# A mixture of 16,384 one-neuron experts on one core: one gather of 8 KB rows per choice, one-hots weighted on VectorE

## The chip, the cores and the metric

The kernel runs on one core of a Trainium2 chip. The core has a matrix engine (TensorE: PE, and PEld for its weight loads), a vector engine (VectorE, DVE), an activation engine (ScalarE, ACT), GpSimd (POOL), and SyncE (SP), which issues most transfers. Each engine works through its own list of instructions in order, and the lists meet only at semaphores. The metric is the time of one execution on the device, in microseconds (us); lower is better.

## The reference

The program is a network of three blocks in float32 over 512 tokens of 1024 features. The change touches only the experts that close the first block. Each of 8 heads picks the best 16 of 128 x 128 experts for a token, so each token has 128 experts; an expert is one row u and one row v of 1024 numbers:

```python
def peer_ffn(a, w_q, sub_keys, u_tab, v_tab):
    qry = (af @ w_q).reshape(n, PEER_HEADS, 2, PEER_KEY_DIM)
    s = jnp.einsum('nhpd,hpkd->nhpk', qry, sub_keys).astype(jnp.float32)
    s_top, i_top = lax.top_k(s, PEER_TOPK)
    cand = (s_top[:, :, 0, :, None] + s_top[:, :, 1, None, :]).reshape(n, PEER_HEADS, PEER_TOPK * PEER_TOPK)
    sc, ci = lax.top_k(cand, PEER_TOPK)
    e_a = jnp.take_along_axis(i_top[:, :, 0], ci // PEER_TOPK, axis=-1)
    e_b = jnp.take_along_axis(i_top[:, :, 1], ci % PEER_TOPK, axis=-1)
    experts = e_a * PEER_N_KEYS + e_b
    gw = jax.nn.softmax(sc, axis=-1)
    ...
        u = u_tab[eb]
        act = jax.nn.gelu(jnp.einsum('td,tkd->tk', xb, u).astype(jnp.float32), approximate=False)
        wts = (gb * act).astype(v_tab.dtype)
        return jnp.einsum('tk,tkd->td', wts, v_tab[eb])
```

## The kernel before

**Two ways to the same sum.** The first 128 tokens (tile 0) are done sparsely: for each of a token's 128 choices the row u is gathered and multiplied with the token (a *dot*, L1508, on DVE), and later the row v is gathered and added with its weight (an *add*, L1513, on DVE). One gather (L1495, issued by POOL) fetches 128 rows, one per token. The other 384 tokens (tiles 1 to 3) are done densely: all 16,384 experts are computed for all of them, 128 experts at a step. A *u-step* computes gelu(u x) (24 matmuls of 384 columns), a *v-step* adds v times the weighted result into six accumulators (18 matmuls of 512). Between the two, the result `at` is multiplied by `gt`, which holds for each expert and token the weight, or zero for an expert that was not chosen.

**How G, the table of weights, is made.** For four tokens at a time DVE writes a one-hot `oa` of each choice's upper index and a one-hot `ob` of the lower (L1609), POOL multiplies `ob` by the weights (L1611), and PE forms four 128 x 128 products in `pa` (L247), which ACT copies to `gs`; 16 tokens of it go to memory `gd` at once. 384 tokens make 96 such groups of four.

**Products.** Each float32 product is three passes over a high and a low part. The weight (512 KB a step) arrives as `wr`, ACT writes its high part `wh` (L227), DVE subtracts to get `wl` (L228); one such subtract a u-step and one a v-step, so 256 in all here. The weighted result is split in the same way, `pwh` on ACT and `pwl` on DVE.

**Two stages.** In the first, 64 of the 128 u-steps run (results to memory) while `peer_select` makes the choices and G: for each head and tile `cand` (L1556) and its 16 largest by two rounds of MAX8, FIND_INDEX8 and MATCH_REPLACE8, then for each half of a choice a decode (L1583 to L1589). In the second, 128 v-steps run with the other 64 u-steps and the gathers: first 64 turns of u and v together (a *pair*), then 64 of v alone. In what follows a *unit* is one u-step or one v-step. At the end `entry` adds the accumulators to x, normalises each tile, transposes it, and begins the next block.

**Who sets the order.** Program order is only a proposal: the scheduler of the block writes out each engine's list by a model of its own, so steps of `peer_gathered`, `peer_select` and the u-steps can be moved past each other within the limits of the pools (`oh`, `pg`, `gr`, `vw` and so on give the number of buffers).

Of the kernel before, what the change touches and what calls it, by code (L numbers as in the profile page):

```python
# [9 lines left out]
F32 = mybir.dt.float32  # L10
F32R = mybir.dt.float32r
BF16 = mybir.dt.bfloat16
# [9 lines left out]
T = 512  # L22
NT = 4
# [64 lines left out]
def pack(I):  # L88
# [35 lines left out]
    g["peer_ur"] = a["peer_u"][0]  # L124
# [49 lines left out]
class Build:  # L174
# [1224 lines left out]
    def peer(self, x, xa, xr, dst):  # L1399
# [13 lines left out]
        with self.pools(pr=1, gr=3) as (pr, gr):  # L1413
            sel = {k: pr.tile([128, 128], d, name=f"sel_{k}") for k, d in (("g", F32), ("e", I32), ("w", F32))}
            with self.pools(pk=1) as pk:
# [8 lines left out]
                with self.pools(uo=3) as uo:  # L1424
                    fill = self.peer_select(vals, idx, iob, gd, sel)
                    for e in range(split):
# [7 lines left out]
            sparse = self.peer_gathered(x, xr, sel, gr)  # L1434
            self.banks(pl=2, pa=0, po=0, pt=0, pv=6)
            acc = [self.psum("pv") for _ in range(6)]
            with self.pools(vg=2, va=2, vw=5) as (vg, va, vw):
                gts, ats, ws = {}, {}, {}

                def first(e):  # L1440

                    if e % 8 == 0:
                        gts[0] = vg.tile([128, n // 16, 8, 16], F32, name="gt")
                        nc.sync.dma_start(gts[0], gd[:, :, e:e + 8].rearrange("c b a t -> b c a t"))
# [8 lines left out]
                    nc.gpsimd.tensor_mul(av, av, gts[0][:, :, e % 8])  # L1453
# [26 lines left out]
            if dst is not None:  # L1480
                self.entry(x, dst, total, True)
            else:
                for t in range(NT):
                    total(t)
        self.ps_open.close()

    def peer_gathered(self, x, xr, sel, gr, ahead=2):
# [3 lines left out]
        w = sel["w"]  # L1491

        def row(table, k):
            r = gr.tile([128, D], F32, name="row")
            nc.gpsimd.indirect_dma_start(  # L1495
                out=r, out_offset=None, in_=table,
                in_offset=bass.IndirectOffsetOnAxis(ap=sel["e"][:, k:k + 1], axis=0))
            return r

        def rows(table):  # L1500
            q = [row(table, k) for k in range(ahead)]
            for k in range(128):
                if k + ahead < 128:
                    q.append(row(table, k + ahead))
                yield k, q.pop(0)

        for k, r in rows(A["peer_ur"]):
            nc.vector.scalar_tensor_tensor(r, r, 1.0, xr, op0=ALU.mult, op1=ALU.mult, accum_out=w[:, k:k + 1])  # L1508
            yield
        nc.scalar.activation(w, w, AF.Gelu)  # L1510
        nc.vector.tensor_mul(w, w, sel["g"])
        for k, r in rows(A["peer_v"].rearrange("a b d -> (a b) d")):
            nc.vector.scalar_tensor_tensor(x[:, 0], r, w[:, k:k + 1], x[:, 0], op0=ALU.mult, op1=ALU.add)  # L1513
            yield
# [28 lines left out]
    def peer_select(self, vals, idx, iob, gd, sel):  # L1543
# [3 lines left out]
        with self.pools(pa=1, pb=2, pg=2, oh=3) as (pa, pb, pg, po):  # L1547
            io16 = iob[:, :16]
            eab = pa.tile([128, 2, T - 128], BF16, name="eab")
            gw = pa.tile([128, T - 128], F32, name="gwt")  # L1550
            for t in (1, 2, 3, 0):
# [47 lines left out]
                nc.vector.tensor_copy(eab[:, :, c], tr[:, :256].rearrange("p (k t) -> p k t", k=2))  # L1599
                nc.vector.tensor_copy(gw[:, c], tr[:, 256:384])  # L1600
                yield
                for u in range(8 * t - 8, 8 * t):
                    gs = pg.tile([128, 128, 16], F32, name="gs")
                    for v in range(0, 16, 4):
                        tok = slice(16 * u + v, 16 * u + v + 4)
                        oa = po.tile([128, 4, 128], F32, name="oa")
                        ob = po.tile([128, 4, 128], F32, name="ob")
# [4 lines left out]
                        ps = self.psum("pa")  # L1612
                        for j in range(4):
                            self.mm1(ps[:, j * 128:j * 128 + 128], ob[:, j], oa[:, j])
# [70 lines left out]
```

## Time and profile before

| | |
|---|---|
| median of three runs | 4912.75 us (4909.2 to 4914.09) |
| the profiled execution | 4902.1 us, of which the span of the trace is 4900.3 us |
| granted TensorE clock, mean | 0.988 |
| PE, DVE, ACT, POOL busy over the span | 96%, 59%, 38%, 19% |
| first stage of the experts | 1044 to 1431 us |
| second stage | 1431 to 2278 us |
| from the last v-step to the next block's first product | 2278 to 2303 us |

The shares of busy time are a mean over stages with different limits; the experts fill a quarter of the span. The end of the second stage is the end of the last v-step on PE. "Start to start" below means the time from the start of an instruction to the start of the next on its engine: neighbours on DVE overlap by 0.07 to 0.08 us in the records, so it is shorter than an instruction's length.

### The profile page before, as it was taken

The numbers are of one execution on the slowest core, as the hardware profiler recorded it, in microseconds if no ns is written. First come the engines' busy times: TensorE is split into PE (matmuls) and PEld (weight loads), VectorE is DVE, ScalarE is ACT, GpSimd is POOL, SyncE is SP. The second block draws the span as 40 slices with busy tenths as digits, with TensorE's granted clock in tenths as the row PEclk, the third lists the DMA queues.
The fourth block names the chain that finished last, engine by engine and source line by source line (L and its number), as shares of the span: only waits on it lengthen the run. The fifth ranks groups of instructions, "written<-read, shape, count | busy, mean of one in ns | idle before, by whom it ended". The sixth has DMA issues, their size and how long they took to land.

```text
span 4900.3 us, 60845 instructions
## 1 busy us (share of the span) xinstructions
PE 4723.5 (96%) x23351; PEld 3983.2 (81%) x23351; DVE 2909.6 (59%) x4764; ACT 1864.6 (38%) x2787; POOL 939.5 (19%) x770
## 2 busy tenths in 40 slices
PE   8999999999999999998999999999999999999999
PEld 7887778799889888777778877887887888887887
DVE  8756655699987777886653355433433433547434
ACT  4576534334433333333442234222322334653222
POOL 0004320004455555663010011000000000001000
PEclk9999999999999999999999999999999999999999
DMA  3445452345589889996222342332332223234332
GB/s 126 129 129 173 140 176 87 112 130 181 189 270 319 309 309 312 333 319 220 84 85 94 97 136 82 101 93 90 103 95 95 88 74 128 88 115 155 103 98 78
DMA packets 299012, 740.16 MB, mean 151 GB/s; under 512 B 26144, under 2 KB 126273, under 8 KB 295521
## 3 DMA queue, kind: packets, MB, share of 16 engines
q1 hardware_dynamic: 261856, 602.04, 38.0%
q0 software_dynamic: 36864, 134.23, 7.6%
q8 instruction: 184, 3.01, 0.3%
q14 instruction: 108, 0.88, 0.1%
HBM read 666.11 MB, written 70.06 MB: 150 GB/s over the span
## 4 chain that ended last, share of the span: by engine, by line
PE 67%; DVE 11%; POOL 7%; issue 7%; DMA 6%; ACT 2%; SPq 0%; POOLq 0%; DVEq 0%; ACTq 0%
PE pl L241 19%; PE pl L243 19%; PE pl L242 19%; POOL row L1495 3%; DMA row<-peer_v,sel_e 3%; PE pt L326 2%; DVE wl L228 2%; PE po L247 2%; POOL at L1453 1%; DVE ob L1609 1%; PE pa L247 1%; DMA wr<-peer_v 1%; DVE oa L1609 1%; PE pv L242 1%; PE pv L243 1%
## 5 line engine op out<-in xcount | busy, mean ns | idle before, releaser
L227 ACT ACTIVATE wh<-wr 128x1024 fp32r<-128x1024 f32 (+3 forms) x836 | 872.0, 1048 | 1657.8 <-PE pl L242 746.5
L228 DVE TENSOR_TENSOR wl<-wr,wh 128x1024 fp32r<-128x1024 f32 (+3 forms) x816 | 1012.3, 1243 | 759.3 <-ACT wh L227 721.1
L241 PE MATMUL pl<-xah,wh 128*128 128x512 f32 (+2 forms) x2448 | 896.5, 366 | 0.1
L243 PE MATMUL pl<-xah,wl 128*128 128x512 f32 (+2 forms) x2448 | 892.8, 365 | 0.7 <-DVE wl L228 0.7
L242 PE MATMUL pl<-xal,wh 128*128 128x512 f32 (+2 forms) x2448 | 891.5, 364 | 0.0
L243 PEld LDWEIGHTS pl<-xah,wl 128*128 128x128 f32 x2448 | 464.0, 190 | 49.7 <-DVE wl L228 1.4
L241 PEld LDWEIGHTS pl<-xah,wh 128*128 128x128 f32 x2448 | 464.2, 190 | 48.9 <-issue 0.9
L242 PEld LDWEIGHTS pl<-xal,wh 128*128 128x128 f32 x2448 | 464.2, 190 | 47.8 <-issue 0.7
L243 PE MATMUL pv<-wh,pwl 128*128 128x512 f32 x768 | 306.3, 399 | 15.4 <-DVE pwl L228 15.4
L242 PE MATMUL pv<-wl,pwh 128*128 128x512 f32 x768 | 305.1, 397 | 1.7 <-DVE wl L228 1.5
L241 PE MATMUL pv<-wh,pwh 128*128 128x512 f32 x768 | 283.9, 398 | 20.8 <-ACT pwh L227 14.5
L228 POOL TENSOR_TENSOR wl<-wr,wh 128x1024 fp32r<-128x1024 f32 x20 | 54.1, 2718 | 1290.6 <-ACT wh L227 1290.6
L242 PE MATMUL pl<-xbl,wh 128*128 128x512 f32 (+1 forms) x752 | 287.3, 382 | 0.8 <-DVE xbl L228 0.8
L241 PE MATMUL pl<-xbh,wh 128*128 128x512 f32 (+1 forms) x752 | 287.1, 382 | 0.0
L243 PE MATMUL pl<-xbh,wl 128*128 128x512 f32 (+1 forms) x752 | 287.0, 382 | 0.0
L243 PE MATMUL pl<-wh,fl 128*128 128x512 f32 x704 | 273.0, 394 | 2.9 <-DVE fl L228 2.9
L241 PE MATMUL pl<-wh,fh 128*128 128x512 f32 x704 | 275.7, 392 | 0.0
L242 PE MATMUL pl<-wl,fh 128*128 128x512 f32 x704 | 274.1, 390 | 0.0
L242 PE MATMUL pl<-wl,xah 128*128 128x512 f32 (+3 forms) x704 | 262.3, 373 | 2.4 <-DVE wl L228 2.4
L241 PE MATMUL pl<-wh,xah 128*128 128x512 f32 (+3 forms) x704 | 261.9, 373 | 1.2 <-ACT xah L684 0.9
L243 PE MATMUL pl<-wh,xal 128*128 128x512 f32 (+3 forms) x704 | 260.3, 370 | 0.0
L424 DVE TENSOR_TENSOR sg<-sg,pl 128x512 f32<-128x512 f32 x88 | 60.5, 687 | 296.9 <-PE pl L243 294.8
(547 smaller groups left out, 8864.2 us busy)
## 6 DMA issues: line engine op xcount, KB each, us to landing
wr<-peer_u SPq DMA_DIRECT2D x128, 512.0 KB, 4.2
wr<-peer_v SPq DMA_DIRECT2D x128, 512.0 KB, 6.4
wr<-ffn_g SPq DMA_DIRECT2D x88, 512.0 KB, 3.5
wr<-ffn_u SPq DMA_DIRECT2D x88, 512.0 KB, 3.7
wr<-ffn_d SPq DMA_DIRECT2D x88, 512.0 KB, 3.5
scratch<-fo SPq DMA_DIRECT2D x96, 256.0 KB, 2.6
scratch<-gs SPq DMA_DIRECT2D x24, 1024.0 KB, 6.3
gt<-scratch SPq DMA_DIRECT2D x16, 1536.0 KB, 12.0
```

The costliest lines, as they stand in the source:

```text
L227: self.nc.scalar.activation(h, src, AF.Copy)
L228: (eng or self.nc.vector).tensor_sub(l, src, h.bitcast(F32))
L241: mm(ps, a[0], b[0], start=start, stop=False)
L242: mm(ps, a[0], b[1], start=False, stop=False)
L243: mm(ps, a[1], b[0], start=False, stop=stop)
L247: self.nc.tensor.matmul(ps, a, b, start=start, stop=stop)
L326: self.nc.tensor.transpose(ps[:rows, i * 128:(i + 1) * 128], s, self.ident)
L424: nc.vector.tensor_mul(pr, pr, ps)
L1453: nc.gpsimd.tensor_mul(av, av, gts[0][:, :, e % 8])
L1495: nc.gpsimd.indirect_dma_start(out=r, out_offset=None, in_=table, in_offset=bass.IndirectOffsetOnAxis(ap=sel["e"][:, k:k + 1], axis=0))
L1609: nc.vector.tensor_tensor(o, iob[:, None, :].to_broadcast([128, 4, 128]), eab[:, k, tok, None].to_broadcast([128, 4, 128]), op=ALU.is_equal)
```

## The change

One table `peer_uv` holds u and v of an expert side by side (8 KB a row), so one gather of the 128 choices serves dot and add: 128 gathers and not 256. Dot k is followed by gelu and weight for that choice alone on ACT, and add k stands one step after dot k. The gathers begin in the first stage, as soon as tile 0 has its choices (tile 0 now comes first), and their share in a step goes by the step's length. 80 u-steps stand in the first stage and 48 in the second, in runs of eight steps that alternate between fresh ones (u and v) and kept ones (v alone). `ob` is written with its weight by DVE, one token at a time with two per-partition scalars; the multiply of `at` by `gt` moves from POOL to DVE. The products of a group are issued two groups later. `gd` is written in pieces of 512 B and read in pieces of 12 KB (before: written in 8 KB, read in 512 B). POOL keeps only the gathers.

```diff
-        n, split = T - 128, 64
+        n, split = T - 128, 80
-        gd = self.dtile([n // 16, 128, 128, 16])
+        gd = self.dtile([16, 128, n // 16, 128])
-        with self.pools(pr=1, gr=3) as (pr, gr):
+        with self.pools(pr=1, gr=(4, "right")) as (pr, gr):
...
+            sparse = self.peer_gathered(x, xr, sel, gr)
+            def gather(share):
+                nonlocal due
+                due += share
+                while due >= 1.0:
+                    due -= 1.0
+                    next(sparse, None)
...
-                        for _ in range(3):
+                        steps += 176.0 / split
+                        while taken < int(steps):
                             next(fill, None)
+                            taken += 1
+                        if taken > 20:
+                            gather(24.0 / (split - 9))
...
-            with self.pools(vg=2, va=2, vw=5) as (vg, va, vw):
+            with self.pools(vg=2, va=2, vw=6) as (vg, va, vw):
...
-                        nc.sync.dma_start(gts[0], gd[:, :, e:e + 8].rearrange("c b a t -> b c a t"))
+                        nc.sync.dma_start(gts[0], gd[e // 8].rearrange("b c (a t) -> b c a t", t=16))
-                    nc.gpsimd.tensor_mul(av, av, gts[0][:, :, e % 8])
+                    nc.vector.tensor_mul(av, av, gts[0][:, :, e % 8])
...
-                order = list(range(split, 128)) + list(range(split))
+                runs, fresh, kept = [], list(range(split // 8, 16)), list(range(split // 8))
+                while fresh or kept:
+                    runs.append((fresh if len(fresh) * (split // 8) >= len(kept) * (16 - split // 8) and fresh else kept or fresh).pop(0))
+                order = [8 * r + i for r in runs for i in range(8)]
+                units = sum(2 if e >= split else 1 for e in order)
                 for i in range(128):
                     first(order[i])
-                    if 2 <= i < 125:
-                        second([i - 2])
-                    for _ in range(2):
-                        next(sparse, None)
+                    if 3 <= i < 126:
+                        second([i - 3])
+                    gather((2 if order[i] >= split else 1) * 106.0 / units)
...
+        for k in range(3):
+            row(k)
+        last = None
+        for k in range(128):
+            r, c = q.pop(0), w[:, k:k + 1]
+            nc.vector.scalar_tensor_tensor(r[:, :D], r[:, :D], 1.0, xr, op0=ALU.mult, op1=ALU.mult, accum_out=c)
+            nc.scalar.activation(c, c, AF.Gelu)
+            nc.scalar.activation(c, c, AF.Copy, scale=sel["g"][:, k:k + 1])
+            if last is not None:
+                add(k - 1, last)
+            last = r
+            if k + 3 < 128:
+                row(k + 3)
             yield
...
-        with self.pools(pa=1, pb=2, pg=2, oh=3) as (pa, pb, pg, po):
+        with self.pools(pa=1, pb=2, pg=2, oh=5) as (pa, pb, pg, po):
-            for t in (1, 2, 3, 0):
+            for t in range(NT):
...
-                        for o, k in ((oa, 0), (ob, 1)):
-                            nc.vector.tensor_tensor(o, iob[:, None, :].to_broadcast([128, 4, 128]),
-                                                    eab[:, k, tok, None].to_broadcast([128, 4, 128]), op=ALU.is_equal)
-                        nc.gpsimd.tensor_tensor(ob, ob, gw[:, tok, None].to_broadcast([128, 4, 128]), op=ALU.mult)
...
+                    nc.vector.tensor_tensor(oa, iob[:, None, :].to_broadcast([128, 4, 128]),
+                                            ea[:, tok, None].to_broadcast([128, 4, 128]), op=ALU.is_equal)
+                    for j in range(4):
+                        i = 4 * q + j
+                        nc.vector.tensor_scalar(ob[:, j], iob, ebg[:, 0, i:i + 1], ebg[:, 1, i:i + 1],
+                                                op0=ALU.is_equal, op1=ALU.mult)
+                    ahead.append((u, v, oa, ob))
+                    if len(ahead) > 2:
+                        product(*ahead.pop(0))
```

Where the scheduler puts it shows in the lists of the engines. The first place is DVE at the start of the one-hots in the first stage; before, the list reads there:

```order
L1567 TENSOR_TENSOR g<-g,s_10257 128x128
L1609 TENSOR_TENSOR oa<-iob,eab 128x512
L1609 TENSOR_TENSOR ob<-iob,eab 128x512
L228 TENSOR_TENSOR wl<-wr,wh 128x1024
L1588 TENSOR_TENSOR oh<-oh,ib 128x256 x4
L1538 MAX_INDEX ci<-sc,cand 128x8 x2
```

and after the change, at the first group of tile 1 (L1643 writes `oa`, L1647 the four parts of `ob`; L1527 is a dot, L1521 an add):

```order
L228 TENSOR_TENSOR wl<-wr,wh 128x1024
L1527 SCALAR_TENSOR_TENSOR row,sel_w<-row,xr 128x1024
L1521 SCALAR_TENSOR_TENSOR x<-row,sel_w,x 128x1024
L1560 MAX_INDEX ci<-sc,cand 128x8 x2
L1643 TENSOR_TENSOR oa<-iob,ea 128x512 x5
L1647 TENSOR_SCALAR ob<-iob,ebg 128x128 x20
L1643 TENSOR_TENSOR oa<-iob,ea 128x512
L1647 TENSOR_SCALAR ob<-iob,ebg 128x128 x4
```

The last two rows go on alternating until all 32 groups of the tile are written: a solid block with no `wl` in it, where before one to three groups stood between two `wl`. There are three such blocks, one for each dense tile, with no, two and one `wl` inside. Between them the list holds the selection, the `wl` of the u-steps, and 59 of the 128 dots and adds: 17 ahead of the first block, 21 between the first two, 16 between the last two, the rest at the third.

The second place is PE at the same point. Before (`pl` is a u-step, L247 forms G):

```order
L241 MATMUL pl<-xah,wh 128x384
L242 MATMUL pl<-xal,wh 128x384
L247 MATMUL pa<-oa,ob 128x128 x4
L243 MATMUL pl<-xah,wl 128x384
L241 MATMUL pl<-xah,wh 128x384
L242 MATMUL pl<-xal,wh 128x384
```

and after:

```order
L241 MATMUL pl<-xah,wh 128x384
L242 MATMUL pl<-xal,wh 128x384
L247 MATMUL pa<-oa,ob 128x128 x12
L241 MATMUL pl<-xah,wh 128x384
L242 MATMUL pl<-xal,wh 128x384
L247 MATMUL pa<-oa,ob 128x128 x116
L243 MATMUL pl<-xah,wl 128x384
```

The 128 products of a tile stand together on PE too, with two matmuls of a u-step between them in the first block, 52 in the second and none in the third. The 80 u-steps stand 39 ahead of the first block, 25 between the first two, 2 inside the second and 14 ahead of the third.

The third place is DVE in the second stage. Before, the list there holds an add with nearly each `wl` up to the last one:

```order
L1513 SCALAR_TENSOR_TENSOR x<-row,sel_w,x 128x1024
L228 TENSOR_TENSOR pwl<-at,pwh 128x384
L228 TENSOR_TENSOR wl<-wr,wh 128x1024
L1513 SCALAR_TENSOR_TENSOR x<-row,sel_w,x 128x1024
L228 TENSOR_TENSOR wl<-wr,wh 128x1024
L1513 SCALAR_TENSOR_TENSOR x<-row,sel_w,x 128x1024 x3
L1479 TENSOR_TENSOR x<-x,pv 128x512 x2
```

After, a dot and an add stand with each `wl` in the first part of the stage (L1467 is the multiply by `gt`, now on DVE):

```order
L1527 SCALAR_TENSOR_TENSOR row,sel_w<-row,xr 128x1024
L228 TENSOR_TENSOR pwl<-at,pwh 128x384
L228 TENSOR_TENSOR wl<-wr,wh 128x1024
L1521 SCALAR_TENSOR_TENSOR x<-row,sel_w,x 128x1024
L1527 SCALAR_TENSOR_TENSOR row,sel_w<-row,xr 128x1024
L228 TENSOR_TENSOR wl<-wr,wh 128x1024
L1521 SCALAR_TENSOR_TENSOR x<-row,sel_w,x 128x1024
L1467 TENSOR_TENSOR at<-at,gt 128x384
```

and none in the rest, where the list reads:

```order
L228 TENSOR_TENSOR wl<-wr,wh 128x1024 x5
L1467 TENSOR_TENSOR at<-at,gt 128x384
L228 TENSOR_TENSOR pwl<-at,pwh 128x384
L228 TENSOR_TENSOR wl<-wr,wh 128x1024 x2
L1467 TENSOR_TENSOR at<-at,gt 128x384
```

What moved is the end of the gathers: 72 dots and 69 adds stand beside the next 66 `wl`, by which point 71 of the stage's 176 units (48 u-steps and 128 v-steps) have their weights, and the last 105 units have none. The normalising of tile 0 stands ahead of the last v-steps.

## Rows read from the trace of the kernel before

**Rows 1.** Busy time by engine in stretches; PEclk, DMA share, GB/s at the end.
```profile
1050.00:1100.00 50.00, 50.00 (x290) 49.97 (x290) 49.80 (x139) 20.27 (x28) 0.00 (x0) 1.00 0.55 178
1106.00:1379.00 273.00, 255.16 (x1639) 244.57 (x1638) 271.09 (x482) 114.08 (x173) 124.05 (x87) 0.99 0.55 186
1431.00:1970.00 539.00, 517.86 (x2563) 463.40 (x2562) 389.60 (x468) 173.33 (x244) 304.02 (x232) 0.99 0.90 312
1475.00:1600.00 125.00, 125.00 (x634) 113.81 (x633) 92.23 (x124) 42.63 (x59) 70.26 (x55) 1.00 0.91 319
1970.00:2278.00 308.00, 290.72 (x1249) 236.34 (x1247) 247.47 (x213) 104.62 (x142) 193.03 (x141) 0.98 0.90 316
2050.00:2075.00 25.00, 25.00 (x112) 20.69 (x112) 24.28 (x20) 9.08 (x12) 20.18 (x14) 1.00 0.99 352
2278.00:2303.00 25.00, 12.44 (x41) 7.92 (x40) 17.79 (x21) 12.90 (x21) 7.33 (x12) 0.59 0.27 89
```

**Rows 2.** Engine waits by waiting line and releaser, 1106 to 1431 us: total, times, longest.
```profile
PE pa L247 <- POOL ob L1611: 23.0, 27, 3.4
DVE row L1508 <- DMA row<-peer_ur,sel_e: 3.8, 4, 1.9
```

**Rows 3.** The same view, 1431 to 2278 us.
```profile
ACT pwh L227 <- POOL at L1453: 335.1, 68, 8.5
DVE row L1508 <- DMA row<-peer_ur,sel_e: 60.3, 46, 5.3
```

**Rows 4.** Instructions by line, POOL 1106:1379 and DVE 1106:1370: busy us, mean ns.
```profile
L1611 POOL TENSOR_TENSOR ob<-ob,gwt 128x512 f32<-128x512 f32 x84 | 120.9, 1442 | 324.2 <-DVE ob L1609 289.4 <-PE pa L247 23.6 <-PE pl L242 3.1
...
L228 DVE TENSOR_TENSOR wl<-wr,wh 128x1024 fp32r<-128x1024 f32 x39 | 53.1, 1361 | 0.0
```

**Rows 5.** DVE's timeline before the one-hots: start, length, instruction.
```profile
1077.98 1.20 DVE L1583 TENSOR_TENSOR oh<-pf,iob 128x1024 bf16<-128x1024 bf16 x1
1079.11 0.73 DVE L1540 MAX8 sc<-cand 128x8 f32<-128x256 f32 x2
1079.77 1.20 DVE L228 TENSOR_TENSOR wl<-wr,wh 128x1024 fp32r<-128x1024 f32 x1
1080.90 0.88 DVE L1588 TENSOR_TENSOR oh<-oh,ib 128x256 bf16<-128x256 bf16 x4
1081.71 0.21 DVE L1577 CAST pf<-pi 128x128 bf16<-128x128 uint32 x1
1081.84 0.07 DVE L1541 MATCH_VALUE_LOAD ci<-sc,cand 128x8 f32 x1
...
1082.64 1.19 DVE L1589 TENSOR_REDUCE e<-oh 128x64 f32<-128x1024 bf16 x1
1083.76 0.40 DVE L1556 TENSOR_TENSOR cand<-vals 128x256 f32<-128x256 f32 x1
```

**Rows 6.** DVE lines: length min/median/max in ns, first and last start.
```profile
L1556 DVE TENSOR_TENSOR cand<-vals x32: 392/411/1258, 1044.3 to 1304.4; 128x256 f32<-128x256 f32 x32
...
L1609 DVE TENSOR_TENSOR oa<-iob,eab x96: 631/679/1522, 1105.9 to 1420.1; 128x512 f32<-128x512 bf16 x96
...
L1508 DVE SCALAR_TENSOR_TENSOR row<-row,xr x128: 1206/1224/3090, 1379.0 to 1798.8; 128x1024 f32<-128x1024 f32 x128
```

**Rows 7.** DVE's timeline: a scalar read per partition (L393), and the last add (L1513).
```profile
201.04 0.28 DVE L393 TENSOR_SCALAR rel<-rel,smr 128x128 f32<-128x128 f32 x1
...
2271.04 1.28 DVE L1513 SCALAR_TENSOR_TENSOR x<-row,sel_w,x 128x1024 f32<-128x1024 f32 x1 [1.17 <-DMA row<-peer_v,sel_e]
```

**Rows 8.** Chain that ended last, 1150 to 1170: a group's products.
```profile
1163.79 2.07 PE pa L247 x8
```

**Rows 9.** DMA issues: how many, KB each, median us from issue to landing.
```profile
scratch<-gs SPq DMA_DIRECT2D x24, 1024.0 KB, 6.3
gt<-scratch SPq DMA_DIRECT2D x16, 1536.0 KB, 12.0
```

**Rows 10.** DMA rate in 40 equal slices, 1970 to 2270 us.
```profile
GB/s 327 287 285 326 342 393 232 387 374 281 325 394 404 253 385 397 297 231 397 282 352 341 103 334 398 257 352 311 400 374 247 262 316 400 268 405 172 401 302 228
```

More of the change, by code (lines that the diff above doesn't have):

```diff
@@ L1479, in total @@
                     nc.vector.tensor_add(o, o, acc[2 * t - 2 + h])
[L1480 to L1484, printed above, removed]
+        if dst is not None:
+            dst = dst()
+            self.entry(x, dst, total, True)
+        else:
+            for t in range(NT):
+                total(t)
         self.ps_open.close()
-    def peer_gathered(self, x, xr, sel, gr, ahead=2):
+        return dst
@@ L1490, in peer_gathered, with row @@
+    def peer_gathered(self, x, xr, sel, gr):
         nc, A = self.nc, self.A
-        w = sel["w"]
-        def row(table, k):
-            r = gr.tile([128, D], F32, name="row")
+        w, q = sel["w"], []
+        def row(k):
+            r = gr.tile([128, 2 * D], F32, name="row")
             nc.gpsimd.indirect_dma_start(
-                out=r, out_offset=None, in_=table,
+                out=r, out_offset=None, in_=A["peer_uv"],
                 in_offset=bass.IndirectOffsetOnAxis(ap=sel["e"][:, k:k + 1], axis=0))
-            return r
@@ L1500, in rows @@
[L1500 to L1508, printed above, removed]
-            yield
-        nc.scalar.activation(w, w, AF.Gelu)
-        nc.vector.tensor_mul(w, w, sel["g"])
@@ L1512, in peer_gathered, with add @@
[L1512 to L1514 removed]
+            q.append(r)
+        def add(k, r):
+            nc.vector.scalar_tensor_tensor(x[:, 0], r[:, D:], w[:, k:k + 1], x[:, 0], op0=ALU.mult, op1=ALU.add)
+        for k in range(3):
[11 more added lines that the diff above has]
+                row(k + 3)
+            yield
@@ L1516, in peer_scores @@
+        add(127, last)
     def peer_scores(self, x, vals, idx, pool):
@@ L1546, in peer_select @@
         nc = self.nc
-        with self.pools(pa=1, pb=2, pg=2, oh=3) as (pa, pb, pg, po):
+        with self.pools(pa=1, pb=2, pg=2, oh=5) as (pa, pb, pg, po):
             io16 = iob[:, :16]
-            eab = pa.tile([128, 2, T - 128], BF16, name="eab")
-            gw = pa.tile([128, T - 128], F32, name="gwt")
-            for t in (1, 2, 3, 0):
+            ea = pa.tile([128, T - 128], BF16, name="ea")
+            ebg = pa.tile([128, 2, T - 128], F32, name="ebg")
+            gs = {}
+            for t in range(NT):
                 sc = pa.tile([128, 8, 16], F32, name="sc")
@@ new lines, in peer_select, with product @@
+                ahead = []
+                def product(u, v, oa, ob):
+                    if v == 0:
+                        gs[0] = pg.tile([128, 128, 16], F32, name="gs")
+                    ps = self.psum("pa")
+                    for j in range(4):
+                        self.mm1(ps[:, j * 128:j * 128 + 128], ob[:, j], oa[:, j])
+                    nc.scalar.activation(gs[0][:, :, v:v + 4], ps.rearrange("p (t a) -> p a t", t=4), AF.Copy)
+                    if v == 12:
+                        nc.sync.dma_start(gd[:, :, u].rearrange("g b k -> b g k"),
+                                          gs[0].rearrange("b (g a) t -> b g (a t)", g=16))
@@ new lines, in peer_select @@
+                for q in range(32 * t - 32, 32 * t):
+                    u, v = q // 4, 4 * (q % 4)
+                    tok = slice(4 * q, 4 * q + 4)
+                    oa = po.tile([128, 4, 128], F32, name="oa")
+                    ob = po.tile([128, 4, 128], F32, name="ob")
+                    nc.vector.tensor_tensor(oa, iob[:, None, :].to_broadcast([128, 4, 128]),
+                                            ea[:, tok, None].to_broadcast([128, 4, 128]), op=ALU.is_equal)
+                    for j in range(4):
+                        i = 4 * q + j
[4 more added lines that the diff above has]
+                        product(*ahead.pop(0))
+                    yield
@@ L1619, in first_block @@
+                for a in ahead:
+                    product(*a)
     def first_block(self, goes_on):
```

25 lines of the change are left out of this document (8 added, 17 removed).

## The prediction

> **What bounds the kernel now.** I read the busy time by stretches first, then the waits, then the instructions of the engine that the waits name. In the first stage DVE is full: 271 of 273 us, and 49.8 of 50 [rows 1]. PE is nearly full beside it, 255 of 273 us, and its losses are waits for POOL's weighted one-hots [rows 2]. So DVE and PE are level there, and what DVE gains in work sets the end. In the second stage PE is the fullest, 518 of 539 us and 291 of 308; the DMA engines are at 0.90, DVE at 390 of 539 and 247 of 308 [rows 1]. What ends last there is seen in the waits: ACT's split stands for POOL's multiply 68 times [rows 3], and DVE for gathered rows [rows 3].
>
> The unit of PE's work comes from the same windows. In 1050 to 1100 PE ran 290 matmuls without a gap, 24 to a u-step: 4.14 us. In 1475 to 1600 it ran 634, 42 to a pair: 8.28 us. In 2050 to 2075 it ran 112, 18 to a v-step: 4.02 us [rows 1]. The second stage before needs 64 x 8.28 + 64 x 4.02 = 787 of its 847 us, so 60 are lost.
>
> **DVE in the first stage, priced start to start.** A `wl` costs 1.13 to 1.14, a MAX8 0.33, a FIND_INDEX8 with its load 0.40, a MATCH_REPLACE8 the same, `cand` 0.33; a list of sixteen is then 0.33 + 2 x 0.33 + 2 x 0.40 + 0.40 = 2.2. A decode is 1.13 + 0.81 + 1.12 = 3.06 [rows 5]. A one-hot of 512 is 0.679 long less its overlap of 0.08: 0.60; a dot has the length of a `wl`, 1.22 against 1.20, so 1.14 [rows 6]; an add is 1.28 less 0.08: 1.20 [rows 7].
>
> The new `ob` has no row. The nearest are of the same 128 columns: a CAST without a scalar per partition, 0.21 long, next start after 0.13 [rows 5], and a TENSOR_SCALAR with one such scalar, 0.28 long, so 0.20 [rows 7]. The new one has two. From below it costs 0.13; from above 0.27, if the second scalar costs what the first did. It is nearest to the row with one scalar, and I take 0.22. Four of them, 0.88, take the place of one 512-wide `ob` at 0.60 and of POOL's multiply.
>
> [...]
>
> The sum: 80 `wl` 91; 96 `oa` 58; 384 parts of `ob` 84; 59 dots 67; 59 adds 71; 32 lists 70, 16 decodes 49 and 8 for the small rest: 498. To this I add 10 for waits: for gathered rows DVE waited only 3.8 us over its first 13 dots [rows 2] but 60 us in 46 waits over those of the second stage [rows 3], and the gathers now run all through the first stage; G's writes are the other candidate. Bounds for the waits are 0 and 28. The selection begins at 1044 [rows 6], so the stage ends at 1044 + 508 = 1552; with the ends of `ob` alone 1517 and 1571. Before it was 1431, but with 16 u-steps fewer, which PE needs 66 us for: like for like DVE loses 55 us.
>
> In this sum the prices are those without GpSimd beside. Before, POOL spent 121 us on 84 multiplies in 1106 to 1379, and there a `wl` took 1361 ns [rows 4] against 1.20 us alone [rows 5]. Priced as above, the rows of DVE from 1044 to its first dot at 1379 come to 291 us and took 335: 44 us of stretch, which POOL's removal gives back. It is in the 498 already; without it the stage would end near 1596.
>
> PE needs 80 x 4.14 + 96 x 1.03 = 430 us there (a group's products took 2.07 for eight records, two to a product [rows 8]), so it idles some 70 us more than it could. It shows where: each solid block takes 32 x 1.48 = 47 us on DVE and 33 on PE, and PE has hardly a u-step beside the first and the third. Having the products two groups behind hides POOL's old wait of 23 us [rows 2] but not this.
>
> **The second stage.** PE needs 48 x 8.28 + 80 x 4.02 = 719 us, 68 less than before. It has 176 units of 4.08. The lists split it. In the first part stand 71 units with 72 gathers. PE needs 290 us there. DVE needs 72 x 1.14 + 69 x 1.20 + 66 x 1.14 for dots, adds and `wl`, 240, and some 55 steps of multiply and `pwl` at 0.47 each (priced by columns between 0.20 for 128 and 0.60 for 512), 52: 292. The DMA has to bring 66 weights of 0.524 MB, 72 gathers of 1.049 MB, and 16.5 MB of G and of u-results: 126.6 MB. A stretch at a share of 0.99 moved 352 GB/s [rows 1], so 360 us, and 16 less for 5.7 MB that the free buffers take in ahead: 344. The best single slice, 405 GB/s [rows 10], gives 297. I take 335, a fifth of the way from the sustained rate, since a row of 8 KB is one piece where two were. So the DMA engines set this part, and PE loses 45 us.
>
> In the rest, 105 units, no gather is left; PE sets the pace, 428 us at 4.08, with about half of today's transfers. Moving the multiply off POOL puts 0.47 us a step on DVE, which then has some 1.14 + 0.94 in 4 to 8 us: hidden. The 335 us of ACT's waits for POOL [rows 3] mostly covered nothing, since PE lost only 60 in all; without the cover of a free DVE the multiply would cost its 128 x 0.47 = 60 us.
>
> The last v-step then ends at 1552 + 335 + 428 = 2315, 37 after today's 2278. **The tail** of 25 us, of which PE is busy 12.4 [rows 1], begins with the last add at 2271 behind a gathered row [rows 7]. Afterwards tile 0 is normalised before the v-steps end, and the other tiles lie on the path as now: 9 less, between 0 and 12. Net +28: 4902 + 28 = 4930 for an execution like the profiled one, and by its distance to the median (10.6) **4941**.
>
> **Rivals.** (A) is the sum above; its own range, with the ends of the waits and of the tail, is 4923 to 4960.
>
> (B) Faster: DVE's and the DMA's new work is cheaper than its nearest rows. If `ob` costs the price without scalars, 0.13, the first stage ends 35 us earlier; if 8 KB rows move near the best slice, the second loses up to 38 less. With the first and half of the second the net is +28 - 35 - 19 = -26, 4887; with both in full -45, 4868. For it: CAST's row, and the many slices near 400. Against it: the L393 row, and DMA windows of 0.90 share that held only 312 to 316 GB/s. It decides for faster where the two save over 38 us together. [...]
>
> (C) Slower still: G's writes pace the blocks. A write of 16 tokens landed after 6.3 us in pieces of 8 KB; 1536 KB in pieces of 512 B landed after 12.0 [rows 9], which is 8.0 for 1024 KB. Two buffers fill in 5.9 us each, so beyond a landing of 5.9 ACT's copies wait, then PE, then DVE through its five one-hot buffers. 2.1 us for 18 of the 24 writes (the first two of each block are free) is 38, of which 10 are in the sum: 4969. Against it: the reads ran among full queues, the writes would run at a share of about 0.6.
>
> (D) Just one half of (B) happens: -7 or -10 against before, 4903 to 4906, no change that shows.
>
> **How the numbers follow.** A 0.42, B 0.28, C 0.18, D 0.12. A measurement of this kernel tells about 0.2%, 10 us, from no change; A and C lie beyond it, B before it, D inside: faster 0.28, same 0.12, slower 0.60. The range leaves out the lower part of B and the upper end of C: 4878 to 4990.
>
> **What would show it.** Right: the first stage ends near 1550 with DVE at 1.00; PE has three holes of 14 us or more beside the blocks; an `ob` part starts 0.20 to 0.25 after the last; DMA share above 0.95 until about 1890, near 0.5 after, and PE dense in the last 430 us; POOL without elementwise work and `wl` back at 1.20. Wrong: `ob` at 0.13; the first part of the second stage under 310 us; or ACT's copies to `gs` waiting for the DMA. What would upset all of it is gathers that land so late in the first stage that the dots, queued in DVE's order ahead of `wl` and `ob`, hold both.

## The result, and the profile after

The changed kernel takes 4958.33 us in the median (4953.63 to 4962.19 over four runs) against 4910.98 of before in the same runs: ratio 1.0098, interval 1.008 to 1.0115. It is 47 us slower; the forecast was 28, and 4941. The profiled execution has a span of 4956.6 us, 56.3 more than before's. The page of the profile, busy time, answers to the shares given ahead:

```profile
PE 4733.1 (95%) x23351; PEld 3990.3 (81%) x23351; DVE 2904.7 (59%) x5179; ACT 1927.7 (39%) x3042; POOL 468.5 (9%) x418
```

DVE's total has not moved at all (2909.6 before), POOL's has halved. So the shares hide the change; the stretches show it. Busy time by engine, with PEclk, DMA share and GB/s at the end, for the first stage, the part of the second with gathers, and the rest:

```profile
1049.00:1565.00 516.00, 442.77 (x2639) 423.49 (x2638) 504.34 (x1159) 206.51 (x378) 88.47 (x59) 0.97 0.80 277
1565.00:1900.00 335.00, 297.62 (x1362) 252.29 (x1361) 292.75 (x382) 130.91 (x278) 98.77 (x69) 0.96 0.97 379
1900.00:2339.00 439.00, 439.00 (x2086) 382.32 (x2086) 216.46 (x271) 163.12 (x223) 5.19 (x12) 1.00 0.53 177
```

In the first, DVE is busy 504 of 516 us and PE waits 73. In the second the DMA share is 0.97 and PE waits 37, with the clock a little lower. In the third PE never waits and nothing else is near full. Compare [rows 1]: before, PE waited 18 of 273 us in the first stage, and 21 of 539 and 17 of 308 in the second. Inside the first stage, PE's holes lie beside the solid blocks and ahead of the third:

```profile
1200.00:1250.00 50.00, 36.82 (x254) 32.13 (x253) 50.00 (x155) 19.47 (x32) 0.94 (x1) 1.00 0.62 190
1490.00:1565.00 75.00, 41.92 (x270) 37.47 (x271) 75.00 (x194) 26.61 (x51) 6.92 (x5) 0.84 0.68 217
```

The first block, and the third with the 15 us ahead of it: DVE 100%, PE 13 of 50 and 33 of 75 us without work. Beside the three blocks PE's gaps come to 15, 10 and 15 us; 18 more lie ahead of the third, where PE has few u-steps left and stands for DVE's selection and one-hots. DVE's timeline in the first block (start, length) gives the price that had no row:

```profile
1201.21 3.10 DVE L1643 TENSOR_TENSOR oa<-iob,ea 128x512 f32<-128x512 bf16 x5
1204.21 5.23 DVE L1647 TENSOR_SCALAR ob<-iob,ebg 128x128 f32<-128x128 bf16 x20
1209.33 0.71 DVE L1643 TENSOR_TENSOR oa<-iob,ea 128x512 f32<-128x512 bf16 x1
```

Twenty parts from 1204.21 to 1209.33: 0.256 each, start to start, against 0.20 with one scalar and 0.13 without [rows 5, 7]. Who waits for whom, 1049 to 1565 us (total, times, longest), answers to [rows 2]:

```profile
ACT gs L1634 <- PE pa L247: 85.3, 85, 4.0
...
PE pa L247 <- DVE ob L1647: 42.4, 65, 7.8
...
DVE row L1527 <- DMA row<-peer_uv,sel_e: 3.5, 3, 2.5
```

PE's wait for POOL (23.0) is now one for DVE (42.4). ACT's copies to `gs` wait for products and never for a write of G, and DVE hardly for a gathered row. The end, on PE's timeline:

```profile
2338.71 0.39 PE L243 MATMUL pv<-wh,pwl 128*128 128x512 f32 x1
2338.94 1.03 PE L326 MATMUL pl<-c_sq,xn 128*128 128x128 f32 x8
...
2358.45 0.80 PE L241 MATMUL pl<-wh,coh 128*128 128x512 f32 x1 [1.83 <-ACT wh L227]
```

The last v-step is over at 2338.9, and the next block's product starts 19.5 us later, where before it was 25.

### The profile page after: what moved, and what is told of

The parts are those of the page before. It is cut to its first block, busy times and chain, and to the rows that moved or that the text cites. A ratio compares the mean times of both kernels' runs of the same rounds, so it can differ in the third digit from the quotient of the medians.

```text
span 4956.6 us, 60668 instructions
## 1 busy us (share of the span) xinstructions
PE 4733.1 (95%) x23351; PEld 3990.3 (81%) x23351; DVE 2904.7 (59%) x5179; ACT 1927.7 (39%) x3042; POOL 468.5 (9%) x418
## 4 chain that ended last, share of the span: by engine, by line
PE 62%; DVE 10%; DMA 3%; issue 2%; ACT 2%; POOL 1%; SPq 0%; POOLq 0%; DVEq 0%; ACTq 0%
PE pl L241 16%; PE pl L243 16%; PE pl L242 16%; PE pv L242 3%; PE pv L243 3%; PE pv L241 3%; DVE ob L1647 2%; DVE wl L228 2%; PE pt L326 1%; PE po L247 1%; DVE x L1521 1%; DVE oa L1643 1%; DVE row L1527 1%; DMA wr<-peer_v 1%; DMA wr<-peer_u 1%
## 5 line engine op out<-in xcount | busy, mean ns | idle before, releaser
L228 DVE TENSOR_TENSOR wl<-wr,wh 128x1024 fp32r<-128x1024 f32 (+3 forms) x816 | 996.6, 1224 | 879.2 <-ACT wh L227 841.2
L241 PE MATMUL pv<-wh,pwh 128*128 128x512 f32 x768 | 264.7, 395 | 28.6 <-ACT wh L227 27.5
L1515 POOL DMA_INDIRECT row<-peer_uv,sel_e x128 | 187.2, 1463 | 767.2 <-DVE x L1521 564.4
```

The lines of the kernel that those rows point to most:

```text
L228: (eng or self.nc.vector).tensor_sub(l, src, h.bitcast(F32))
L241: mm(ps, a[0], b[0], start=start, stop=False)
L1515: nc.gpsimd.indirect_dma_start(out=r, out_offset=None, in_=A["peer_uv"], in_offset=bass.IndirectOffsetOnAxis(ap=sel["e"][:, k:k + 1], axis=0))
```

## The experiments

The question of the forecast was the two places where it put the loss. Theory M: the first stage ends when DVE's list is worked off, in whatever order, and the second loses where gathers and weights fill the DMA engines. Rival S: the loss is the solid blocks. Other rivals are named with their runs. Times are medians in us, with the ratio to the kernel before on the same chip.

| run | us | ratio, interval |
|---|---|---|
| e1_no_lag | 4994.71 | 1.0184, 1.0166 to 1.0201 |
| e2_tile0_last | 4897.82 | 0.9978, 0.9968 to 0.9987 |
| e3_ob_weight_on_act | 4978.97 | 1.0148, 1.0131 to 1.0165 |
| e4_ob_weight_on_pool | 5028.25 | 1.0242, 1.0225 to 1.0259 |
| e5_tile0_last_paced | 4897.88 | 0.9980, 0.9970 to 0.9989 |
| e6_before_tile0_first | 5050.26 | 1.0295, 1.0278 to 1.0312 |
| e7_before_ob_on_dve | 4918.33 | 1.0028, 1.0017 to 1.0040 |
| e8_tile0_last_ob_on_act | 4898.64 | 0.9978, 0.9968 to 0.9988 |
| e9_no_gathers | 4798.0 | 0.9775, 0.9759 to 0.9792 |
| e10_paced_by_fresh_steps | 4903.32 | 0.9992, 0.9981 to 1.0002 |
| e11_tile0_last_third_buffer | 4902.34 | 0.9990, 0.9980 to 0.9999 |
| e12_half_the_bytes | 4815.27 | 0.9815, 0.9795 to 0.9835 |

**Are the solid blocks the loss?**

```diff
-        with self.pools(pa=1, pb=2, pg=2, oh=5) as (pa, pb, pg, po):
+        with self.pools(pa=1, pb=2, pg=2, oh=3) as (pa, pb, pg, po):
-                    if len(ahead) > 2:
+                    if len(ahead) > 0:
```

> The changed kernel with the products of a group issued at once (no two-group lag) and three one-hot buffers instead of five. The solid blocks of 32 groups go: one to three groups stand between two weight subtracts for tiles 1 and 2 (52 groups still stand together at the end). The list of DVE holds 69 dots and 67 adds in the first stage instead of 56 and 54. Theory M (the amount of DVE's work in the first stage sets its end, in whatever order): first stage 30 us longer, its PE idle time spread, 13 gathers fewer behind it (13.6 MB at 379 GB/s, 36 us): 4958 within 12 us. Rival S (the loss is that PE has no u-steps beside the solid blocks): the holes of PE close, 40 to 60 us faster, 4900 to 4918.

It became 36 us slower than the changed kernel. Two of its stretches:

```profile
1200.00:1300.00 100.00, 94.73 (x609) 93.86 (x609) 94.62 (x214) 46.62 (x81) 11.79 (x8) 1.00 0.89 292
...
1450.00:1500.00 50.00, 17.18 (x79) 15.29 (x78) 48.68 (x101) 12.79 (x30) 12.75 (x10) 0.60 0.78 259
```

The holes of the first block closed and came back later: with the u-steps used up, PE stands beside a full DVE at a clock of 0.60. The last one-hot starts at 1591.9 instead of 1559.9, 32 us later, as 13 dots and adds more at 2.34 should make it. Rival S falls. But M's other half fails too: the 13 gathers that were gone from the second stage gave nothing back. Its part with gathers is 46 us shorter (289 for 335), but PE did fewer units in it, 1134 matmul records against 1362, and waited the same 37 us. PE's rows show where. In the changed kernel 34 of the 37 us lie in two stretches of v-steps alone (14 of them) that have gathers beside them; a third such stretch, after the gathers, takes 58 us and not 77 or 83:

```profile
1621.00:1698.00 77.00, 62.36 (x256) 48.85 (x255) 65.27 (x88) 26.68 (x57) 22.42 (x16) 0.93 0.99 392
1776.00:1859.00 83.00, 63.94 (x256) 48.81 (x255) 67.19 (x89) 28.18 (x60) 23.29 (x16) 0.94 0.97 375
2032.00:2090.00 58.00, 58.00 (x258) 48.02 (x257) 30.73 (x40) 20.31 (x28) 0.00 (x0) 1.00 0.69 246
```

In e1 the gathers still reach over two such stretches, and they cost the same:

```profile
1655.00:1736.00 81.00, 61.94 (x253) 48.81 (x252) 67.31 (x91) 28.24 (x62) 25.25 (x17) 0.92 0.97 375
1815.00:1893.00 78.00, 62.49 (x255) 48.36 (x254) 62.91 (x82) 28.35 (x56) 14.03 (x10) 0.96 0.88 340
```

So in these two kernels the loss went with the number of such stretches that the gathers met, and not with the number of gathers left. The first of them moved 30.2 MB (77 us at 392 GB/s); to do that in 58 us it would have taken 520 GB/s, an estimate from the first and the third row.

**Do the early gathers cost?** In e2 the tiles go 1, 2, 3, 0 and no gather stands in the first stage; e6 puts the opposite into the kernel before, by one line.

```diff
-            for t in range(NT):
+            for t in (1, 2, 3, 0):
...
-                            gather(24.0 / (split - 9))
+                            pass
...
-                    gather((2 if order[i] >= split else 1) * 106.0 / units)
+                    gather((2 if order[i] >= split else 1) * 130.0 / units)
```

> The changed kernel with tile 0's choices made last (tiles 1, 2, 3, 0, as in the kernel before) and no gathers in the first stage's program order, so that no dot or add can stand in the first stage. 110 dots and adds leave DVE's list there, 129 us. Theory M: the first stage then ends by PE's 430 us and not by DVE's 500: near 1480 to 1490 instead of 1565; the second stage has all 128 gathers, 134 MB of some 267 MB, 704 us at 379 GB/s against 719 us that PE needs, so 740 to 770 us instead of 774; in all 4855 to 4890, faster than the kernel before. Rival D (the DMA engines set the sum over both stages): what the first stage gains the second loses, 4940 to 4960. Rival S expects a gain too, since the one-hots then stand mixed, but no more than in e1_no_lag.

```diff
-            for t in (1, 2, 3, 0):
+            for t in range(NT):
```

> The kernel before with one line changed: tile 0's choices are made first, as in the changed kernel. The scheduler then puts 126 of the 128 dots into the first stage, where 10 stood. Theory M (early dots lengthen a first stage whose DVE is full, and the second stage has at most 60 us to give back): first stage 116 x 1.14 = 132 us longer, second up to 60 shorter: 4970 to 5000. Rival (the early gathers fill DVE's and the DMA engines' slack and are not what costs in the changed kernel): 4890 to 4925.

e2 is 60 us faster than the changed kernel and 0.2% faster than the one before. The size was off, for the second stage took more than expected:

```profile
1050.00:1400.00 350.00, 350.00 (x2280) 349.79 (x2279) 341.33 (x933) 157.16 (x232) 0.00 (x0) 1.00 0.66 201
1434.00:2050.00 616.00, 544.75 (x2492) 463.50 (x2491) 534.93 (x689) 244.96 (x511) 185.48 (x124) 0.96 0.97 377
2050.00:2250.00 200.00, 200.00 (x959) 175.18 (x958) 97.64 (x125) 75.04 (x103) 2.28 (x4) 1.00 0.52 178
```

The first stage is now without a loss on PE (350 of 350), with DVE at 0.98 behind it. All that is lost is lost from 1434 to 2050, at a DMA share of 0.97: PE waits 71 us.

e6 is 142 us slower than before, past the forecast:

```profile
1050.00:1600.00 550.00, 412.07 (x2222) 390.79 (x2220) 534.34 (x928) 153.62 (x228) 314.23 (x225) 0.79 0.74 249
...
1450.00:1500.00 50.00, 20.42 (x83) 17.43 (x83) 46.54 (x70) 5.97 (x10) 32.13 (x23) 0.53 0.59 198
```

The last one-hot pair starts at 1596 where it was 1420 [rows 6], 176 us later, not the 132 of the dots alone. Two candidates for the 44 more are POOL's multiplies, which still run beside, and PE's clock at 0.53. DVE's instructions by line, 1105 to 1597 us, speak for the first:

```profile
L1508 DVE SCALAR_TENSOR_TENSOR row<-row,xr 128x1024 f32<-128x1024 f32 x126 | 169.8, 1358 | 14.0 <-DMA row<-peer_ur,sel_e 13.9
```

DVE stood still for 14 of 549 us, and nearly all of that was for gathered rows, so it did not wait for a slow PE. A dot took 1.36 us in the mean and a one-hot 0.91, where before a dot took 1.22 in the median [rows 6] and a one-hot 0.78 in the mean: some 16 and 26 us more. That POOL is what stretches them is inferred, by the comparison of e3 and e4 below. From the last one-hot pair to the end of the last v-step it takes 835 us, where before it took 858: of the 176 paid early, 23 come back.

**The weight of the one-hot, on three engines.**

```diff
-                    for j in range(4):
-                        i = 4 * q + j
-                        nc.vector.tensor_scalar(ob[:, j], iob, ebg[:, 0, i:i + 1], ebg[:, 1, i:i + 1],
-                                                op0=ALU.is_equal, op1=ALU.mult)
+                    nc.vector.tensor_tensor(ob, iob[:, None, :].to_broadcast([128, 4, 128]),
+                                            ebg[:, 0, tok, None].to_broadcast([128, 4, 128]), op=ALU.is_equal)
+                    for j in range(4):      # e3; e4: one multiply of 128x512 by nc.gpsimd
+                        nc.scalar.activation(ob[:, j], ob[:, j], AF.Copy, scale=ebg[:, 1, 4 * q + j:4 * q + j + 1])
```

> The changed kernel with the lower one-hot as one 128x512 comparison on DVE and its weight applied by ScalarE, four multiplies of 128x128 with a scalar per partition. DVE loses 384 x 0.257 - 96 x 0.60 = 41 us; the scheduler then puts 18 dots and adds more into the first stage (42 us), and mixes the blocks of tiles 1 and 2. Theory M: first stage as long as now (1565 within 10), 18 gathers fewer behind it, so the second stage 25 to 45 us shorter: 4913 to 4935. Rival S: 30 to 60 us more gain from the mixed blocks, under 4905. A rival of its own: ScalarE, whose 384 multiplies take at least 0.25 us each, 96 us, becomes late with the high parts; then no gain, 4950 or more.

> The changed kernel with the lower one-hot as one 128x512 comparison on DVE and its weight applied by GpSimd, as in the kernel before. The order of DVE is close to that of the run with ScalarE (73 dots and 71 adds in the first stage, blocks of tiles 1 and 2 mixed). If GpSimd's two-input work stretches DVE's, as the 44 us for 84 multiplies in the kernel before were read, it is 45 to 55 us slower than the run with ScalarE: 4958 to 4985. If that stretch was something else, the two runs are the same within 10 us.

e3 misses: 21 us slower than the changed kernel. The scheduler filled the 41 us with dots and adds, so the first stage was no shorter (last one-hot at 1568.8), and again the fewer gathers left for later did not pay: PE waited 40 us beside them. The result also lies where the expectation's own rival, a late ScalarE, put it (4950 or more). The trace gives that rival a part: DVE waited 12 us for ACT's high parts, 7 in the changed kernel. How the rest of the 21 divides is open. Between e3 and e4 lie 49 us, the forecast of 45 to 55; the profiled executions, e3's the fastest of its runs and e4's the slowest, lie 61 apart, and their last one-hots 62. Instructions by line on DVE show where (busy us, mean ns), e3:

```profile
L228 DVE TENSOR_TENSOR wl<-wr,wh 128x1024 fp32r<-128x1024 f32 x46 | 56.3, 1225 | 11.7 <-ACT wh L227 11.5
```

and e4:

```profile
L228 DVE TENSOR_TENSOR wl<-wr,wh 128x1024 fp32r<-128x1024 f32 x46 | 70.1, 1525 | 7.2 <-ACT wh L227 7.2
```

The same `wl` takes 1525 ns beside GpSimd's multiplies and 1225 without. Two more runs follow: in e7 the weighted `ob` on DVE alone is put into the kernel before, and e8 is e2 with the edit of e3, so `ob` is weighted on ACT without early gathers. The edit of e7:

```diff
+            eb = pa.tile([128, T - 128], F32, name="eb")
...
+                nc.vector.tensor_copy(eb[:, c], tr[:, 128:256])
...
-                        nc.gpsimd.tensor_tensor(ob, ob, gw[:, tok, None].to_broadcast([128, 4, 128]), op=ALU.mult)
...
+                        for j in range(4):
+                            i = 16 * u + v + j
+                            nc.vector.tensor_scalar(ob[:, j], iob, eb[:, i:i + 1], gw[:, i:i + 1],
+                                                    op0=ALU.is_equal, op1=ALU.mult)
```

> The kernel before with one part of the change: the weighted one-hot written by VectorE in four parts (two scalars per partition), and GpSimd's multiply of it gone. DVE gains 384 x 0.257 - 96 x 0.60 = 41 us of work and loses the 44 us by which GpSimd's multiplies stretched it. If that reading of the stretch is right: no change within 15 us, 4895 to 4922. If the stretch was something else: 40 us slower, 4940 to 4960.

> The kernel of e2_tile0_last with the lower one-hot compared on DVE in one instruction and weighted by ScalarE. DVE loses 41 us of work in the first stage and takes up 9 dots and 7 adds (19 us). In e2 PE is busy all the time from 1100 to 1400 and DVE at 0.97. Theory M: with no gathers there PE sets the first stage, so DVE's relief gives nothing: within 12 us of e2, 4886 to 4910. Rival (ScalarE's 384 multiplies make the high parts late, as e3 allows): 15 to 40 us slower than e2.

e7 is 10 us slower, within the forecast, but not for its reason. In the first stage the 41 us put on DVE and GpSimd's stretch taken off nearly cancel: the last one-hot starts 21 us earlier (1399 for 1420), and 18 of these are the ten dots, with their wait for rows, that stood ahead of it before and now stand later. The last v-step then ends 13 us earlier (2265 for 2278). The loss comes behind it: the last add ends at 2284, and the next block's product starts 52 us after the last v-step, where before it was 25. So the forecast total is luck, and the balance in the first stage is what bears on the stretch. e8 equals e2: where PE sets the stage, 41 us of DVE are worth nothing.

**What the sparse tile costs, and by what.** In e9 the gathers are left out of the changed kernel, in e12 half of their bytes out of e2's.

```diff
-            sparse = self.peer_gathered(x, xr, sel, gr)
+            sparse = iter(())
...
-                            gather(24.0 / (split - 9))
+                            pass
```

```diff
-                out=r, out_offset=None, in_=A["peer_uv"],
+                out=r[:, :D], out_offset=None, in_=A["peer_v"].rearrange("a b d -> (a b) d"),
...
-            nc.vector.scalar_tensor_tensor(x[:, 0], r[:, D:], w[:, k:k + 1], x[:, 0], op0=ALU.mult, op1=ALU.add)
+            nc.vector.scalar_tensor_tensor(x[:, 0], r[:, :D], w[:, k:k + 1], x[:, 0], op0=ALU.mult, op1=ALU.add)
-            nc.vector.scalar_tensor_tensor(r[:, :D], r[:, :D], 1.0, xr, op0=ALU.mult, op1=ALU.mult, accum_out=c)
+            nc.vector.scalar_tensor_tensor(r[:, D:], r[:, :D], 1.0, xr, op0=ALU.mult, op1=ALU.mult, accum_out=c)
```

> The changed kernel with the gathered rows left out: no gather, no dot and no add, so the first 128 tokens lack their experts' sum. What the sparse tile costs in all. Without dots and adds to place, the scheduler's list no longer has solid blocks (one to five groups between two weight subtracts). Theory M: the first stage ends by PE and the second has no full DMA engines: PE needs 1149 us from 1049, so the last v-step ends near 2205 to 2225 instead of 2339, 114 to 134 us less: 4825 to 4845. Rival (PE also loses by something else of the change: the weighted one-hots on DVE, the multiply on DVE, reads of G and of the u-results): above 4860.

> The kernel of e2_tile0_last with rows of 4 KB instead of 8: each gather brings the v row alone, and dot and add both read it, so tile 0's result lacks u. The number of gathers, DVE's dots and adds and their places by the steps stay as in e2; 67 MB fewer are moved. Theory D (the DMA engines set PE's loss of some 80 us between 1434 and 2050, 267 MB in the stage): the loss falls to 0 to 25 us, 4820 to 4845. Rival V (DVE's 2.34 us for each dot and add, in DVE's order ahead of the low parts, is what makes PE wait): no change, 4885 to 4910; in between, both.

Without gathers PE never waits in the first stage (390 of 390 us from 1044 to 1434), nor from 1434 to 2050:

```profile
1434.00:2050.00 616.00, 616.00 (x2974) 540.57 (x2973) 295.46 (x380) 226.99 (x310) 0.00 (x0) 1.00 0.58 196
```

and the last v-step ends at 2176, earlier than the 2205 to 2225 that was expected. So without the sparse tile beside them the one-hots and the multiply on DVE cost PE nothing, and what the sparse tile costs the changed kernel in all is 160 us of span. In e12, with e2's dots and adds:

```profile
1434.00:2050.00 616.00, 609.82 (x2926) 533.84 (x2926) 575.43 (x751) 274.13 (x556) 201.23 (x124) 1.00 0.83 298
```

DVE is busier than in e2 (575 for 535, as more fits into the stretch), yet PE loses 6 us and not 71. Of the 100 us that lie between e2 and e9, 83 go with half of the bytes and 17 are left. The gathered bytes set e2's second stage, and DVE's work for dots and adds does not; this also speaks against e5's rival below, by which a gather costs PE its own time wherever it stands.

**Can the transfers be spread?** e5 holds the gathers back to the pace of the steps, e10 asks in program order for six times as many gathers in a fresh step as in a kept one, e11 lets the u-results be read earlier. The edits are shown against e2, e5 and e2:

```diff
+                    sel["at"] = a
...
-                    gather((2 if order[i] >= split else 1) * 130.0 / units)
+                    gather((2 if order[i] >= split else 1) * 140.0 / units)
...
+            if k % 4 == 0:
+                nc.vector.scalar_tensor_tensor(sel["e"][:, k:k + 4], sel["at"][:, :4], 0.0, sel["ef"][:, k:k + 4], op0=ALU.mult, op1=ALU.add)
             r = gr.tile([128, 2 * D], F32, name="row")
...
```

```diff
-                    gather((2 if order[i] >= split else 1) * 140.0 / units)
+                    gather((3.0 if order[i] >= split else 0.5) * 134.0 / (3.0 * 48 + 0.5 * 80))
```

```diff
-            with self.pools(vg=2, va=2, vw=6) as (vg, va, vw):
+            with self.pools(vg=2, va=3, vw=6) as (vg, va, vw):
```

> The kernel of e2_tile0_last with its gathers held back: four row numbers at a time are written out by DVE from the newest result of the second stage (times zero), so that gathers cannot run ahead of the steps; 128 gathers then stand beside nine tenths of the second stage's weights instead of two thirds. In e2 PE lost some 82 us between 1434 and 2050 at a DMA share of 0.97 and nothing after. Theory M (the second stage loses where gathers and weights together fill the DMA engines): 25 to 50 us faster than e2, 4848 to 4873. Rival (each gather costs PE its own time, by DVE's order or by landing late, wherever it stands): within 10 us of e2, 4888 to 4908.

> The kernel of e5_tile0_last_paced with another share: a fresh step (pair) takes six times the gathers of a kept step (v alone), while e5 gave them two to one. In e5 PE stayed full in stretches of pairs and lost its time in runs of kept steps, where PE asks for a weight every 4 us and the u-results and G are read beside. Theory D (the DMA engines are full in the kept runs): 15 to 40 us faster than e5, 4858 to 4883. Rival L (the wait is for the first read of u-results in a kept run, which has too few buffers, gathers or not): within 10 us of e5.

> The kernel of e2_tile0_last with a third buffer for the weighted results (va 3 instead of 2), so that the u-results of a kept run can be read four steps earlier. Theory D (full DMA engines): no change, 4888 to 4908. Rival L (late reads into too few buffers make the multiply, and behind it in ACT's order the high parts, late): 15 to 40 us faster than e2, 4858 to 4883.

None of the three gained. e5 missed M's forecast and e10 D's, and both fell within the range of their rival; e11 came out at no change, as D said, which leaves e10's rival L, late reads into too few buffers, without support. In e11 ACT's wait for the multiply falls from 44.2 us to 17.8 and PE's wait for the high parts stays (44.2, now 46.9): the buffers were not it. In e5 the gathers last to 2193 and not 2031, but PE's loss is only moved. A full DMA share alone is not what makes it, as the first of these rows shows beside the second, one of its two worst:

```profile
2050.00:2100.00 50.00, 50.00 (x238) 43.48 (x237) 38.85 (x54) 17.47 (x36) 15.21 (x12) 1.00 0.97 387
2100.00:2150.00 50.00, 37.38 (x145) 29.30 (x144) 40.18 (x59) 16.70 (x37) 11.26 (x8) 0.86 0.96 367
2150.00:2200.00 50.00, 48.05 (x232) 43.08 (x231) 38.29 (x45) 21.56 (x38) 3.82 (x4) 0.97 0.70 242
```

Shares of 0.70 stand next to 0.96: the gathers were spread, the demand still came in bursts. The loss is again in the stretches of v-steps alone, 56 of 68 us (in e2 56 of 71), and the adds in them say why the pace gained nothing: in e2 the three long stretches of 14 v-steps that have gathers hold 16 or 17 adds each, in e5 there are four of 13 to 16.

e10 did not do what it was written for. Its two first such stretches hold 16 and 14 adds, and the first stretch of pairs between them 14: the scheduler did not keep the shares of the program order. The first stretch of v-steps alone, and the pairs behind it:

```profile
1520.00:1601.00 81.00, 63.41 (x256) 48.60 (x255) 67.20 (x91) 29.58 (x63) 21.57 (x17) 0.96 0.97 371
1601.00:1677.00 76.00, 75.38 (x375) 67.35 (x374) 65.77 (x89) 31.98 (x66) 23.29 (x15) 1.00 0.90 344
```

So that gathers kept out of these stretches would cost less is likely by e12 and these rows, but no run shows it.

## Why the prediction was right, point by point

**The sign and the two places** held. The sum said +28, the measurement +47; it lies in the range and near the upper end of the forecast's own case.

**The first stage** was to end at 1552 and ended at 1565. The mis-sized term is `ob`: 0.256 and not 0.22, 384 x 0.036 = 14 us. It fell near the upper bound, which had said that the second scalar costs what the first did. Four parts at 0.256 come to 1.02 for the 0.60 of one 512-wide `ob`, though the four also apply the weight. The stage also began 4.5 us later. Against that, the 59 dots and 59 adds of the sum were 56 and 54 up to the last one-hot, 9 us less. The 10 for waits were about right: DVE was busy 504 of 516 and waited 12, 7 of them for ACT's high parts and 3.5 for gathered rows. The three holes of 14 us came as 15, 10 and 15; the 18 us ahead of the third block were not foreseen.

**GpSimd's stretch** of 44 us for 84 multiplies held in its size: e3 against e4 49 us for 96, and in e7's first stage a near balance.

**The part with gathers** was put at 335 and took 336 (1565 to 1901). The reason given, DMA at its rate, is shown by e12 for e2's second stage, which has the same rows and rate (0.97, 377 GB/s). That the parts of the changed kernel behave alike is inferred from the equal share. That the time came out to 1 us is in part luck: the bytes were summed, but a fifth of the way between two rates was a choice. What the prediction did not have is where PE loses it, in v-steps alone.

**The rest** was 438 (1901 to 2339) and not 428: I counted 105 units by DVE's subtracts, but PE had 106.3 left (656 matmuls of u-steps, 1422 of v-steps), which is 5 us. The other 5 are the price: matmuls of a v-step start every 0.2275 us, so a v-step takes 4.10 us and not the 4.02 of [rows 1], where a window of 25 us counts the matmuls cut at its edges as whole. **The tail** gave 5.7 and not 9.

So 13 + 1 + 10 + 3 = 27 us more than the forecast of 28 makes 55 of the 56 between the profiled executions; the medians, whose kernel before lies higher than its profiled run, differ by 47.

**What I had in mind wrongly.** I took the solid blocks for PE's hole in the first stage. They are where it shows, not why: e1 removed two of three and lost 36 us more. The cause is the amount of DVE's work ahead of the stage's end, above all the early gathers. Nor did I weigh what an early gather returns: 2.34 us of DVE paid in the first stage, and in the second hardly anything (e1, e3, e6), for in e1 as in the changed kernel the gathers left met two stretches of v-steps alone.

**The rivals.** B's cheap `ob` is excluded by the row, its rate of 405 GB/s by 379. C did not come: no copy to `gs` waited for a write. D did not come.

**A version that loses nothing** is e2: the change with tile 0 last, 0.9978 of before. Its gain over before is 11 us, about the 10 that the prediction called a measurement's width, as the second stage loses most of what the first saves beside the gathers.

## What to carry to other kernels

Work that a scheduler pulls forward is paid at the price of the stage that it lands in: ask which engine is full there, and what the later stage, limited by another resource, gives in return. A hole beside a solid block of instructions need not be that block's fault; sum the full engine's list before changing its order. To tell transfer from work, halve the bytes and leave the instructions: here one run settled what three runs on pace and buffers did not. And before a run is read as a test of an order, look in its trace whether the order came about: e10's did not.

## What was not expected of the hardware

A TENSOR_SCALAR of 128 columns with two scalars per partition started 0.256 us after the last; one with one scalar was 0.28 long, so 0.20, and a CAST without one took 0.13, start to start [rows 5, 7]. The three differ in their types too, and no run changed the number of scalars alone, so that it is the scalars that cost is an inference. And in two stretches where PE was starved its clock was lower as well: with 17 of 50 us busy the granted clock was 0.60 in e1, and with 20 of 50 it was 0.53 in e6. In the kernel before, eight 128-column matmuls of L247 took 2.07 us from 1163.79 [rows 8], where the granted clock was 0.50 (1163 to 1169), and 1.05 us from 1171.53, where it was 1.00 (1170 to 1180). What the lower clock added to the times of e1 and e6 was not measured by itself.
